# GpSimd's products of sample histories with taps, first five convolution blocks, set behind the issues of the adding transfers of low parts

## The chip, the core and the metric

The kernel runs on one core of one Trainium2 chip. The core has five engines that run beside each other and wait for one another through semaphores: TensorE (PE in the profile; its weight loads are a row of their own, PEld), VectorE (DVE), ScalarE (ACT), GpSimd (POOL) and SyncE (SP, which here only issues transfers). Sixteen DMA engines move the data. The metric is the time of one execution on the device in microseconds; the time of a kernel is the median of several runs.

## What is computed

One step of a decoder layer over 288 tokens: 256 of a prompt and 8 sequences of 4 new tokens, which carry a history. The part of the reference that the change touches is the depthwise convolution of width 31 over the gated projection; for the samples it runs over 30 tokens of history and the 4 new ones.

```python
h = rmsnorm(x, norm1_g)
proj = einsum("btd,de->bte", h, w_in) + b_in          # 2048 -> 3072
a, gate, z = proj[..., :1024], proj[..., 1024:2048], proj[..., 2048:]
u = a * sigmoid(gate)
u_ext = concatenate([hist_conv, u], axis=1)
c = silu(layernorm(depthwise_causal_conv(u_ext, conv_w, conv_b), ln_g, ln_b))
d = multiscale_pool(concatenate([hist_pool, z], axis=1), pos0)
p = einsum("btgc,gce->btge", d, pool_w) * pool_scale
x = x + einsum("btm,md->btd", concatenate([c, p]), w_out)
h2 = rmsnorm(x, norm2_g)
x = x + einsum("btf,fd->btd", square(relu(einsum("btd,df->btf", h2, w_ff1))), w_ff2)
y = rmsnorm(x, norm_f)
```

## The kernel before

**Products in three parts.** Channels lie on the 128 partitions, the 288 tokens along the free axis. A product in float32 is made from three products of halves: weight and activation are split into a high part (a cast to float32r) and a low part (value minus high part), and `gemm` (L296) adds high x high, low x high and high x low in a PSUM bank. A block of 256 weight columns over 2048 rows so takes 16 x 2 x 3 = 96 matmuls of 128x288. All of them are issued at L291, in the order of the program.

**Stages.** The projection goes by blocks in the order of `SEQUENCE` (L45): convolution blocks c0 to c7 (128 columns of a and 128 of the gate each), pool blocks p3 to p0, and small pool products P3 to P0 between them. c0 and c1 run together first, then c2, c3, c4, p3, c5 and so on. Then come the product with `w_out`, and four rounds of the feed-forward part.

**Weights.** `load` (L164) issues a transfer of 128x4x256 weights into a `wr` tile on SP's queue; six such tiles rotate. `split_part` (L254) makes the two parts: ScalarE casts the tile to `whi` (L260), and the low part `wlo` is made in one of three ways. V: VectorE subtracts (L265). G: GpSimd subtracts, in two halves (L268). D: ScalarE writes the negated high part into `wlo` (L262), and GpSimd issues a transfer that reads the weights again from device memory and adds them onto it (L263), the adding transfer of this text. `whi` and `wlo` have five buffers each. `WAYS` (L73) deals the ways out, four tiles to a block: c2 GVGV, c3 GDGG, c4 GDGD, p3 GDDG, c5 GDGD; the other blocks have no D. There are thus seven adding transfers; this text calls them D1 (c3, second tile), D2 and D3 (c4, second and fourth), D4 and D5 (p3, second and third), D6 and D7 (c5). Of a block's 96 matmuls the first 24 use the first tile, the next 24 the second, and so on; the first use of a tile's low part is the third of its 24.

**The convolution.** `conv_pair` (L427) scales the two banks of a block by the row of norms, makes u, and then, at a far lower priority (`later`, L111), the convolution: for the prompt one ScalarE instruction and 30 steps on VectorE (L445, L448); for the samples GpSimd multiplies all 8 x 4 windows with the 31 taps in one instruction (L451, 128x992, into a `prd` tile, two of which rotate), and VectorE sums them (L453). The results `c` are needed only by the layer norm, whose mean `ln_mean` (L549) enters the matmuls within the `w_out` stage.

**What sets the order.** Each engine runs its instructions in a fixed order, which a scheduler draws up from the dependencies and priorities. `tc.issue_after(x)` makes the scheduler set what is inside behind the instruction `x`. On GpSimd the subtractions, the issues of D1 to D7, the tap products and the pool sums stand in one such row, so a transfer is not issued before the instruction ahead of it has ended.

**Reordered heads.** At eight places (the first block, c2, c5, and later ones) `gemm` gets `classes=`, a string of zeros and ones (`TURN`, L70, 48 of them): it takes the next matmul of the head whose row parity is the digit, so the head's matmuls run in another order. Elsewhere the parity alternates.

Of the kernel before, what the change touches and what calls it, by code (L numbers as in the profile page):

```python
# [12 lines left out]
ALU = mybir.AluOpType  # L13
# [3 lines left out]
P = 128  # L17
D = 2048
SEQ = 256
NB, NS = 8, 4  # L20
# [4 lines left out]
CW = 31  # L25
# [61 lines left out]
def trunk_kernel(ctx: ExitStack, tc: tile.TileContext, io):  # L87
# [3 lines left out]
    nc = tc.nc  # L91
# [14 lines left out]
    def nm(s):  # L106
        seen[s] = seen.get(s, 0) + 1
        return f"{s}{seen[s]}"

    @contextmanager  # L110
    def later(by=LATER):  # L111

        tc.cur_priority += by
        yield
        tc.cur_priority -= by
# [18 lines left out]
    def f32(t):  # L134
        return t.bitcast(F32)
# [5 lines left out]
    def windows(ap, n):  # L141

        (step, parts), (far, groups), (near, size) = ap.ap
        return bass.AP(ap.tensor, ap.offset, [[step, parts], [far, groups], [near, size - n + 1], [near, n]])

    def samples(ap, n):
        return ap.rearrange("p (b t) -> p b t", t=n)
# [8 lines left out]
    def v(key, j):  # L156
        return vec[:, OFF[key] + j : OFF[key] + j + 1]
# [91 lines left out]
        last = mm(psum[:, 0, :T], minus, total, start=True, stop=True)  # L249
        return row_of(psum, psum[:, 0, :T], *args), last  # L250

    turns = {}

    def split_part(raw, src, hi, lo, way):  # L254

        nc.scalar.copy(hi, raw)  # L260
        if way == "D":
            nc.scalar.activation(lo, f32(hi), AF.Copy, scale=-1.0)  # L262
            nc.gpsimd.dma_start(lo, src, accum_op=ALU.add)  # L263
        elif way == "V":
            nc.vector.tensor_tensor(lo, raw, f32(hi), op=ALU.subtract)  # L265
        else:
            for j in range(0, raw.shape[1], 2):
                nc.gpsimd.tensor_tensor(lo[:, j : j + 2, :], raw[:, j : j + 2, :], f32(hi[:, j : j + 2, :]), op=ALU.subtract)  # L268
# [7 lines left out]
    def split(halves, stage="ff"):  # L276

        parts = []
        for raw, src in halves:
            turns[stage] = turns.get(stage, -1) + 1  # L280
            parts.append(spl())
            ways = WAYS.get(stage) or WAYS[stage[0]]
            split_part(raw, src, *parts[-1], ways[turns[stage] % len(ways)])
        return lambda k, m: columns(*parts[k // 4], k % 4, m)
# [88 lines left out]
    def pool_weights(g):  # L373
        raw, (hi, lo) = load_pool(g), spl()
        split_part(raw[:, 0:2, :], None, hi[:, 0:2, :], lo[:, 0:2, :], "V")
        return lambda k, m: columns(hi, lo, k, m)
# [35 lines left out]
    rb = row("rb")  # L412


    cs, pcs = [], []
    sum_c = tmpp.tile([P, 2, T], F32, name="sum_c", tag="ag2", bufs=2)

    def history(i):
# [8 lines left out]
    def conv_pair(i, banks):  # L427
        up = u_all[:, i, 0:UO]
        us = samples(u_all[:, i, UO:UL], US)
        ta, gate = [b[:, :T] for b in banks]  # L430
        for b in (gate, ta):
            nc.vector.tensor_tensor(b, b, rb, op=ALU.mult)
        tg = tmpp.tile([P, 2, T], F32, name=nm("tg"), tag="ag", bufs=2)[:, 0, :]
        nc.scalar.activation(tg, gate, AF.Sigmoid, bias=v("b_in", 8 + i))
        for out, a, b in ((up[:, CH:UO], ta[:, :SEQ], tg[:, :SEQ]), (us[:, :, CH:US], samples(ta[:, SEQ:T], NS), samples(tg[:, SEQ:T], NS))):
            nc.vector.scalar_tensor_tensor(out=out, in0=a, scalar=v("b_in", i), in1=b, op0=ALU.add, op1=ALU.mult)
        if i % 2 == 0:
            cs.append(actp.tile([P, 2, T], F32, name=nm("c"), tag="c", bufs=4))
        c = cs[i // 2][:, i % 2, :]
        with later():  # L440
            if i % 2 == 0:
                pcs.append(cvp.tile([P, 2, SEQ], F32, name=nm("pc"), tag="cv"))
            pc = pcs[i // 2][:, i % 2, :]
            cwv = vec[:, CWO + i * CW : CWO + (i + 1) * CW]
            nc.scalar.activation(pc, up[:, 0:SEQ], AF.Identity, bias=v("conv_b", i), scale=cwv[:, 0:1])  # L445
            for w in range(1, CW):
                dst = pc if w < CW - 1 else c[:, 0:SEQ]
                nc.vector.scalar_tensor_tensor(out=dst, in0=up[:, w : w + SEQ], scalar=cwv[:, w : w + 1], in1=pc, op0=ALU.mult, op1=ALU.add)  # L448
            prd = prdp.tile([P, NB, NS, CW + 1], F32, name=nm("prd"), tag="prd")
            nc.scalar.activation(prd[:, :, :, CW], ones[:, 0 : NB * NS].rearrange("p (b t) -> p b t", t=NS), AF.Identity, bias=v("conv_b", i), scale=0.0)  # L450
            nc.gpsimd.tensor_tensor(prd[:, :, :, 0:CW], windows(us, CW), cwv[:, None, None, :].to_broadcast([P, NB, NS, CW]), op=ALU.mult)  # L451
            cso = c[:, SEQ:T]
            nc.vector.tensor_reduce(samples(cso, NS), prd, axis=AX.X, op=ALU.add)  # L453
            if i % 2 and 1 < i < N8 - 1:
                for m in range(2):
                    nc.gpsimd.tensor_tensor(sum_c[:, m, :], (cs[0] if i == 3 else sum_c)[:, m, :], cs[i // 2][:, m, :], op=ALU.add)
            if i == N8 - 2:
                for part in (sum_c[:, 1, :], c):
                    nc.gpsimd.tensor_tensor(sum_c[:, 0, :], sum_c[:, 0, :], part, op=ALU.add)
# [54 lines left out]
    third = conv_products(2, classes=TURN)  # L514
    nc.gpsimd.memset(z_all[:, :, 0:PH], 0.0)
    conv_pair(0, pair0)
    conv_pair(1, pair1)
    conv_pair(2, third)
    def ahead(n):

# [61 lines left out]
    for j, c in enumerate(cs):  # L582
        n = tmpp.tile([P, 2, T], F32, name=nm("n"), tag="ag", bufs=2)
        nc.vector.tensor_tensor(n, c, norm["rows"][:, None, :].to_broadcast([P, 2, T]), op=ALU.mult)
        for m in range(2):
            i = 2 * j + m
# [195 lines left out]
```

## Time and profile before

| | |
|---|---|
| median of 3 runs | 1081.95 us (1081.67 to 1083.03) |
| profiled execution | 1082.43 us, of which its span 1080.6 us |
| granted TensorE clock | 0.998 |
| instructions in the span | 19528 |
| adding transfers | 7, of 512 KB each |
| tap products on GpSimd | 8, of 128x992 |

The span is the time from the first to the last instruction; the 1.83 us between it and the execution's time lie around it. Rows of the trace give a start in microseconds from the span's beginning, a duration, the engine, the line, the operation with its tiles, and a count; in square brackets stands how long the engine idled just before, and what ended that.

### The profile page before, as it was taken

How to read it: one execution, taken by the hardware profiler on the slowest of the kernel's cores; microseconds unless marked ns; L12 is line 12 of the kernel's file. 1: busy time of each engine (PE TensorE's matmuls, PEld its weight loads, DVE VectorE, ACT ScalarE, POOL GpSimd, SP SyncE). 2: the span in 40 equal slices, each digit the busy share in tenths (PEclk: the TensorE clock that was granted, in tenths of full speed). 3: DMA queues.
4: the chain of work that ended last, by engine and by line, in shares of the span. 5: the costliest groups of instructions: out<-in, count | busy, mean ns of one | idle time of the engine just before them, and what ended most of it. 6: DMA issues, size and time to landing. Idle time of an engine off the chain costs nothing.

```text
span 1080.6 us, 19528 instructions
## 1 busy us (share of the span) xinstructions
PE 1069.2 (99%) x8176; PEld 1067.9 (99%) x8176; DVE 633.7 (59%) x810; ACT 479.0 (44%) x588; POOL 175.9 (16%) x182
## 2 busy tenths in 40 slices
PE   9999999999999999999999999999999999999996
PEld 8999999999999999999999999999999999999996
DVE  7899999788654544444554444555544445554553
ACT  8654445665544433334443333444433334444441
POOL 0878979512000000000000000000000000000001
PEclk9999999999999999999999999999999999999999
DMA  9896478555555555555555555555555555555522
GB/s 326 288 263 182 145 187 247 177 171 173 162 173 166 169 175 163 170 173 165 170 174 164 170 170 167 171 173 162 173 168 167 173 171 164 173 166 170 172 79 88
DMA packets 58296, 190.71 MB, mean 176 GB/s; under 512 B 6240, under 2 KB 11232, under 8 KB 58208
## 3 DMA queue, kind: packets, MB, share of 16 engines
q1 hardware_dynamic: 56336, 184.35, 54.3%
q0 software_dynamic: 1008, 3.67, 1.9%
q8 instruction: 64, 1.05, 0.4%
q10 hardware_dynamic: 864, 1.44, 0.4%
q14 instruction: 24, 0.20, 0.0%
HBM read 185.16 MB, written 4.28 MB: 175 GB/s over the span
## 4 chain that ended last, share of the span: by engine, by line
PE 75%; issue 21%; ACT 2%; POOL 1%; DMA 1%; SPq 0%; POOLq 0%; DVE 0%
PE ac L291 74%; POOL wlo L268 1%; DMA wr<-in_w 1%; ACT whi L349 1%; PE pp L291 1%; DMA wlo<-in_w 1%; ACT hx L354 0%; ACT z_all L405 0%; POOL prd L451 0%; POOL xT L718 0%; ACT whi L260 0%; SPq L191 0%; POOLq L768 0%; DVE xT L691 0%; ACT whi L356 0%
## 5 line engine op out<-in xcount | busy, mean ns | idle before, releaser
L260 ACT CAST whi<-wr 128x1024 fp32r<-128x1024 f32 (+1 forms) x332 | 346.5, 1044 | 551.3 <-PE ac L291 536.7
L265 DVE TENSOR_TENSOR wlo<-wr,whi 128x1024 fp32r<-128x1024 f32 x288 | 353.5, 1227 | 348.1 <-ACT whi L260 348.1
L291 PE MATMUL ac<-ax,whi 128*128 128x288 f32 x2048 | 351.0, 292 | 0.0
L291 PE MATMUL ac<-fx,whi 128*128 128x288 f32 x2048 | 350.2, 292 | 0.0
L291 PEld LDWEIGHTS ac<-ax,whi 128*128 128x128 f32 x2048 | 296.0, 187 | 0.0
L291 PEld LDWEIGHTS ac<-fx,whi 128*128 128x128 f32 x2048 | 295.6, 187 | 0.0
L291 PE MATMUL ac<-ax,wlo 128*128 128x288 f32 x1024 | 217.3, 292 | 0.0
L291 PE MATMUL ac<-fx,wlo 128*128 128x288 f32 x1024 | 216.4, 292 | 0.0
L291 PEld LDWEIGHTS ac<-ax,wlo 128*128 128x128 f32 x1024 | 162.5, 187 | 0.0
L291 PEld LDWEIGHTS ac<-fx,wlo 128*128 128x128 f32 x1024 | 162.2, 187 | 0.0
L291 PE MATMUL ac<-hx,whi 128*128 128x288 f32 x768 | 131.9, 296 | 1.4 <-DVE hx L352 1.4
L718 POOL TENSOR_TENSOR xT<-xT,rf 128x288 f32<-128x288 f32 x4 | 3.1, 795 | 799.9 <-ACT rf L722 799.9
L291 PEld LDWEIGHTS ac<-hx,whi 128*128 128x128 f32 x768 | 112.6, 190 | 1.8 <-ACT hx L354 1.7
L268 POOL TENSOR_TENSOR wlo<-wr,whi 128x512 fp32r<-128x512 f32 x74 | 102.4, 1433 | 17.1 <-ACT whi L260 16.0
L448 DVE SCALAR_TENSOR_TENSOR pc<-u_all,vec,pc 128x256 f32<-128x256 f32 x232 | 99.3, 479 | 1.9 <-ACT pc L445 0.7
L291 PE MATMUL ac<-hx,wlo 128*128 128x288 f32 x384 | 80.4, 295 | 0.2 <-DMA wlo<-in_w 0.2
L291 PEld LDWEIGHTS ac<-hx,wlo 128*128 128x128 f32 x384 | 61.1, 189 | 0.4 <-DMA wlo<-in_w 0.4
L291 PE MATMUL ac<-dx,whi 128*128 128x288 f32 x256 | 46.8, 295 | 0.0
L291 PE MATMUL ac<-mx,whi 128*128 128x288 f32 x256 | 44.9, 293 | 0.0
L660 DVE SCALAR_TENSOR_TENSOR t<-ac,r 128x576 f32<-128x576 f32 x32 | 24.2, 757 | 25.4 <-PE ac L291 25.3
L291 PEld LDWEIGHTS ac<-dx,whi 128*128 128x128 f32 x256 | 38.4, 188 | 0.2
L291 PEld LDWEIGHTS ac<-mx,whi 128*128 128x128 f32 x256 | 37.5, 188 | 0.2 <-DVE xT L579 0.2
(129 smaller groups left out, 529.6 us busy)
## 6 DMA issues: line engine op xcount, KB each, us to landing
wr<-in_w SPq DMA_DIRECT2D x335, 512.0 KB, 3.8
wlo<-in_w POOLq DMA_DIRECT2D x7, 512.0 KB, 7.8
xT<-in_xT SPq DMA_DIRECT2D x8, 288.0 KB, 7.7
wr<-in_w SPq DMA_DIRECT2D x5, 256.0 KB, 3.9
out_u_out<-u_all SPq DMA_DIRECT2D x1, 1208.0 KB, 9.6
u_all<-in_hist_c SPq DMA_DIRECT2D x8, 136.0 KB, 5.3
out_z_out<-z_all SPq DMA_DIRECT2D x1, 668.0 KB, 9.2
z_all<-in_hist_p SPq DMA_DIRECT2D x4, 152.0 KB, 6.6
```

Source lines behind the costliest of these rows:

```text
L260: nc.scalar.copy(hi, raw)
L265: nc.vector.tensor_tensor(lo, raw, f32(hi), op=ALU.subtract)
L268: nc.gpsimd.tensor_tensor(lo[:, j : j + 2, :], raw[:, j : j + 2, :], f32(hi[:, j : j + 2, :]), op=ALU.subtract)
L291: last = nc.tensor.matmul(*args, **kw)
L349: nc.scalar.copy(hi[:, blocks[0]], raw[:, blocks[0]])
L448: nc.vector.scalar_tensor_tensor(out=dst, in0=up[:, w : w + SEQ], scalar=cwv[:, w : w + 1], in1=pc, op0=ALU.mult, op1=ALU.add)
L660: nc.vector.scalar_tensor_tensor(out=t, in0=bk[:, :, :T], scalar=0.0, in1=both(rows2[0]), op0=ALU.max, op1=ALU.mult)
L718: eng.tensor_tensor(xk, xk, r[:, None, :].to_broadcast([P, n, T]), op=ALU.mult)
```

## The change

The list `added` collects the issues of the adding transfers. The tap products of block i are set behind one of them by `issue_after`: those of c0 and c1 behind D1, that of c2 behind D2, those of c3 and c4 behind D4. Since D2 and D4 have to exist by then, the emission of the convolution of c2 and c3 is put off by one block (`waiting`); the body of `conv_pair` from L439 on becomes the function `taps`. Nothing is computed otherwise than before.

```diff
-    turns = {}
+    turns, added = {}, []
...
-            nc.gpsimd.dma_start(lo, src, accum_op=ALU.add)
+            added.append(nc.gpsimd.dma_start(lo, src, accum_op=ALU.add))
...
-    cs, pcs = [], []
+    cs, pcs, waiting = [], [], []
...
+        while waiting:
+            taps(*waiting.pop())
+        if i in (2, 3):
+            waiting.append((i, up, us))
+        else:
+            taps(i, up, us)
+
+    def taps(i, up, us):
+
         c = cs[i // 2][:, i % 2, :]
         with later():
...
-            nc.gpsimd.tensor_tensor(prd[:, :, :, 0:CW], windows(us, CW), cwv[:, None, None, :].to_broadcast([P, NB, NS, CW]), op=ALU.mult)
+            with tc.issue_after(added[max(0, min(3, 2 * i - 3))].ins):
+                nc.gpsimd.tensor_tensor(prd[:, :, :, 0:CW], windows(us, CW), cwv[:, None, None, :].to_broadcast([P, NB, NS, CW]), op=ALU.mult)
```

Lines behind L439 move down by up to ten (L268 and L263 keep their numbers, L451 becomes L461), and the numbers of the tiles of c4 and later blocks change with the order of emission. The first place is GpSimd's row around the first adding transfer. Before, with `wlo_604` and `wlo_609` the low parts of c3's first two tiles, `wlo_618` and `wlo_623` those of the other two, and `prd_667` and `prd_708` the products of c0 and c1:

```order
L268 TENSOR_TENSOR wlo_604<-wr_599,whi_603 128x512 x2
L451 TENSOR_TENSOR prd_667<-u_all,vec 128x32x31
L451 TENSOR_TENSOR prd_708<-u_all,vec 128x32x31
L263 DMA wlo_609<-in_w 128x1024
L268 TENSOR_TENSOR wlo_618<-wr_613,whi_617 128x512 x2
L268 TENSOR_TENSOR wlo_623<-wr_615,whi_622 128x512 x2
```

In the changed kernel the same stretch of GpSimd reads:

```order
L268 TENSOR_TENSOR wlo_604<-wr_599,whi_603 128x512 x2
L263 DMA wlo_609<-in_w 128x1024
L461 TENSOR_TENSOR prd_667<-u_all,vec 128x32x31
L461 TENSOR_TENSOR prd_708<-u_all,vec 128x32x31
L268 TENSOR_TENSOR wlo_618<-wr_613,whi_617 128x512 x2
L268 TENSOR_TENSOR wlo_623<-wr_615,whi_622 128x512 x2
```

D1 has moved ahead of two tap products. The second place follows directly on GpSimd: before, the four tiles of c4 (`wlo_858` to `wlo_877`, D2 and D3 among them), the first three of p3 (`wlo_1027`, then D4 and D5) and the products of c2 and c3 (`prd_751`, `prd_918`):

```order
L268 TENSOR_TENSOR wlo_858<-wr_853,whi_857 128x512 x2
L451 TENSOR_TENSOR prd_751<-u_all,vec 128x32x31
L263 DMA wlo_863<-in_w 128x1024
L268 TENSOR_TENSOR wlo_872<-wr_867,whi_871 128x512 x2
L263 DMA wlo_877<-in_w 128x1024
L268 TENSOR_TENSOR wlo_1027<-wr_1022,whi_1026 128x512 x2
L451 TENSOR_TENSOR prd_918<-u_all,vec 128x32x31
L263 DMA wlo_1032<-in_w 128x1024
L263 DMA wlo_1041<-in_w 128x1024
```

The same rows of the changed kernel, where the tiles have the numbers 822 to 841 for c4, 990 to 1004 for p3, and 883 and 1051 for the products of c2 and c3:

```order
L268 TENSOR_TENSOR wlo_822<-wr_817,whi_821 128x512 x2
L263 DMA wlo_827<-in_w 128x1024
L461 TENSOR_TENSOR prd_883<-u_all,vec 128x32x31
L268 TENSOR_TENSOR wlo_836<-wr_831,whi_835 128x512 x2
L263 DMA wlo_841<-in_w 128x1024
L268 TENSOR_TENSOR wlo_990<-wr_985,whi_989 128x512 x2
L263 DMA wlo_995<-in_w 128x1024
L461 TENSOR_TENSOR prd_1051<-u_all,vec 128x32x31
L263 DMA wlo_1004<-in_w 128x1024
```

D2 and D4 have each moved ahead of one tap product; D3 and D5 stand where they stood, and so do the products of c4 and later blocks. TensorE's order is the same in both kernels, and SP's too but for one output transfer that moves by one place. ScalarE and VectorE run the same instructions with a few swaps of neighbours and another interleaving of the convolution's steps: VectorE runs six steps instead of three before the first sum over a `prd` tile.

## The prediction

> **What bounds the kernel now.** I began with the page's busy times and the list of TensorE's waits.
>
> ```profile
> PE 1069.2 (99%) x8176; PEld 1067.9 (99%) x8176; DVE 633.7 (59%) x810; ACT 479.0 (44%) x588; POOL 175.9 (16%) x182
> PE ac L291 <- DVE hx L352: 1.4, 1, 1.4
> PE warm L214 <- DVE cst L231: 1.0, 1, 1.0
> PE ac L291 <- DMA wlo<-in_w: 0.2, 1, 0.2
> ```
>
> TensorE is busy 99% of the span and waits three times in all. Two of the waits are at the start; the third is for an adding transfer. GpSimd, whose row the change edits, is busy 16%, so its own time is worth nothing; only what it issues can matter. The chain of work that ended last says where:
>
> ```profile
> 44.41 5.97 DMA wlo<-in_w
> 50.38 0.04 issue
> 50.42 60.24 PE ac L291 x454
> ...
> 171.50 26.61 PE ac L291 x204
> ...
> 282.86 572.63 PE ac L291 x4404
> ```
>
> From 50.42 us on the chain is TensorE alone, and just ahead of it stands D1, issued at 44.41 and landed at 50.38. Whatever brings that matmul forward brings the end forward, as long as nothing else becomes late. TensorE's rows around the wait:
>
> ```profile
> 48.77 0.68 PE L291 MATMUL ac<-hx,whi 128*128 128x288 f32 x4
> ...
> 49.55 0.68 PE L291 MATMUL ac<-hx,whi 128*128 128x288 f32 x4
> 50.42 0.54 PE L291 MATMUL ac<-hx,wlo 128*128 128x288 f32 x2 [0.20 <-DMA wlo<-in_w]
> 50.80 0.69 PE L291 MATMUL ac<-hx,whi 128*128 128x288 f32 x4
> 51.59 0.70 PE L291 MATMUL ac<-hx,whi 128*128 128x288 f32 x4
> 52.39 0.70 PE L291 MATMUL ac<-hx,whi 128*128 128x288 f32 x4
> ```
>
> Two things are to be seen. Rows overlap, since matmuls are pipelined, so I read starts and not durations. Ahead of the wait, four high and two low matmuls pass between 48.77 and 49.55: 0.78/6 = 130 ns each. The next one was due at 49.55 + 4 x 0.13 = 50.07 and came at 50.42; it and its neighbour then took 0.38 instead of 0.26. The wait so costs 0.35 + 0.12 = **0.47 us**, more than the 0.20 that the idle time shows. And behind it the step is 0.80 (51.59 to 52.39): 133.3 ns per matmul. The wait has put TensorE into another rhythm. How long this lasts, the view by stages tells (busy time, count, granted clock, share of the DMA engines, GB/s):
>
> ```profile
> 42.00:49.80 7.80, 7.80 (x62) 1.00 0.62 155
> 52.00:84.00 32.00, 32.00 (x243) 1.00 0.97 261
> 95.00:127.00 32.00, 32.00 (x248) 1.00 0.50 156
> 127.00:159.00 32.00, 32.00 (x249) 1.00 0.57 167
> 175.00:191.00 16.00, 16.00 (x125) 1.00 0.84 225
> ```
>
> A window also counts two or three matmuls that stick out at its edges: 32/0.1333 = 240 (243 counted), 32/0.130 = 246 (248). All stages read 100% busy at a granted clock of 1.00, and yet the one behind the wait does fewer matmuls. The slow rhythm ends at c5, whose head is reordered.
>
> **The change, part by part.** GpSimd's row, the waits in brackets, and the two ScalarE rows that write what D1 and D2 add onto:
>
> ```profile
> 37.65 2.55 POOL L268 TENSOR_TENSOR wlo<-wr,whi 128x512 fp32r<-128x512 f32 x2 [2.21 <-ACT whi L260]
> 40.16 4.33 POOL L451 TENSOR_TENSOR prd<-u_all,vec 128x992 f32<-128x992 f32 x2
> 44.41 1.01 POOL L263 DMA_DIRECT2D wlo<-in_w  x1
> 45.21 7.75 POOL L268 TENSOR_TENSOR wlo<-wr,whi 128x512 fp32r<-128x512 f32 x6
> 52.71 2.42 POOL L451 TENSOR_TENSOR prd<-u_all,vec 128x992 f32<-128x992 f32 x1
> 54.86 1.11 POOL L263 DMA_DIRECT2D wlo<-in_w  x1
> ...
> 63.76 2.16 POOL L451 TENSOR_TENSOR prd<-u_all,vec 128x992 f32<-128x992 f32 x1
> 65.99 0.88 POOL L263 DMA_DIRECT2D wlo<-in_w  x1
> 68.90 0.87 POOL L263 DMA_DIRECT2D wlo<-in_w  x1 [2.04 <-ACT wlo L262]
> 39.26 1.06 ACT L262 ACTIVATE wlo<-whi 128x1024 fp32r<-128x1024 f32 x1
> 51.09 1.06 ACT L262 ACTIVATE wlo<-whi 128x1024 fp32r<-128x1024 f32 x1
> 64.38 1.06 ACT L262 ACTIVATE wlo<-whi 128x1024 fp32r<-128x1024 f32 x1
> 67.54 1.06 ACT L262 ACTIVATE wlo<-whi 128x1024 fp32r<-128x1024 f32 x1
> ```
>
> *D1.* ScalarE has its part ready at 39.26 + 1.06 = 40.32, GpSimd is free at 40.20. In the new order the issue goes out at about 40.4, 4.0 us sooner. How long the seven adding transfers take to land:
>
> ```profile
> DMA to landing us min/median/max: 6.0/7.8/10.2
> ```
>
> D1's own 5.97 gives a landing at 46.4, the longest 50.6; the need is at 50.07. The shortest is D1's, at a DMA share of 0.62 (row 42.00:49.80), and its new place lies mostly in the same stretch, so I take 46.4: 3.7 us of slack, and the wait goes. That removes 0.47 us.
>
> *The rhythm.* The matmul at 50.42 is the 27th of c3's 96 (the first low one of its second tile), the one at 50.80 the 29th. From there 68 are left of c3, and 96 each of c4 and p3: 260 matmuls run at 133.3 ns before c5's reordered head, which so begins at 50.80 + 34.66 = 85.46; at 130 ns they save 260 x 3.33 ns = **0.87 us**. Bounds for this term: 0, if the slow rhythm came from something else, and 0.87. The row 42.00:49.80 (62 matmuls, 7.8/0.13 = 60 and two at the edges) shows c2 and the head of c3 running at 130 until the wait and only until it, so I take 0.87.
>
> *Tap products of c0 and c1* start at about 41.4 instead of 40.16 and end near 45.7. Behind them stand the low parts of c3's third tile, done 0.4 us later than before, about 48.2; their first use by TensorE is its third tile's third matmul, 50.07 + 24 x 0.13 = 53.19. Those 5 us hide the delay. VectorE's sums over the products come later too, but with more steps of the convolution ahead of them, and only the layer norm's mean needs them. Both cost nothing.
>
> *D2 and D4* go out one product earlier: D2 when GpSimd has done c4's first tile, at about 53.3 (52.71, and the half microsecond by which the six subtractions now end later) instead of 54.86, D4 at about 65.4 instead of 65.99, since ScalarE's part is ready only at 65.44. *D3 and D5* go out as before, D5 behind ScalarE's 67.54 + 1.06. None of the four is waited for now, so no time is removed. But TensorE now comes sooner and could meet them; that is the first rival.
>
> *VectorE* is the next engine that could be late, as it carries the convolution up to the layer norm's mean.
>
> ```profile
> 85.66 0.76 DVE L470 TENSOR_TENSOR tz<-ac,rb 128x576 f32<-128x576 f32 x1 [0.90 <-PE ac L291]
> ...
> 195.26 0.46 DVE L553 TENSOR_TENSOR sum_c<-pmean,c 128x288 f32<-128x288 f32 x1
> ...
> 197.96 0.65 PE L291 MATMUL pmean<-sum_c,ones 128*128 128x288 f32 x2
> ```
>
> It ends the sum at 195.72, 2.2 us before TensorE takes it up, more than the whole gain; and at 85.66 it idles 0.90 for TensorE, so it will follow when TensorE comes sooner. The cover holds.
>
> **Sum:** 0.47 + 0.87 = 1.34 us. Against the profiled execution's own 1082.43 (span 1080.6 and 1.83 around it) that is 1081.1. That execution is 0.48 above the median of the runs, 1081.95; the same gain taken from the median gives **1080.6 us**.
>
> **A rule against the second term.** In the rows above TensorE makes 130 and 133.3 ns per matmul at one granted clock of 1.00. The Trainium skill, "TensorE: Matmul & The Clock Gate", section "Back-to-back issue gap", gives one isolated gap for a warm clock, columns/2.4 + 2.5 ns, for 288 columns 122.5 (an estimate from that page), with no second rhythm. By that rule a wait costs its gap and no more, and the sum would be 0.47 us. The trace disagrees with it as far as the two rates go. What remains of the rule is that the slow rhythm might follow from something other than the wait; that is a rival below.
>
> **The rivals.**
>
> *The gain is given back at p3.* The rows of D4 and D5 alone:
>
> ```profile
> DMA to landing us min/median/max: 9.8/9.8/9.8
> DMA to landing us min/median/max: 10.2/10.2/10.2
> ```
>
> D5 lands at 68.90 + 10.2 = 79.1. p3 starts at 50.80 + (68 + 96) x 0.1333 = 72.7, and needs D5 with its 51st matmul, at 72.7 + 50 x 0.1333 = 79.3: 0.2 us of slack now. In the new order the need is at 50.07 + (70 + 96 + 50) x 0.13 = 78.15. ScalarE works at TensorE's pace here, which at 67.5 is ahead by 0.47 and (67.5 - 50.8)/0.1333 x 3.33 ns = 0.42, so D5's issue moves by about 0.9 to 68.0, and D5 would land at 78.2 if it took 10.2 again. For a shorter time speaks that D1 and D2 have left the crowded stretch (0.97 of the DMA engines between 52 and 84) by 4.0 and 1.6 us. Against it, that the stretch stays nearly full and TensorE draws on it 2.5% faster. If D5 were 0.6 late, the wait and 46 matmuls of slow rhythm (0.15) would come back: 1081.4.
>
> *One rhythm.* Only the gap goes: 1081.95 - 0.47 = 1081.5.
>
> *The change doesn't do what it says.* D1 takes 10.2 at its new place, lands at 50.6, and the wait stays: 1082.0.
>
> *Slower: the reordered head of c5.* It now finds TensorE in the slow rhythm and leaves it in the fast one. In the changed kernel it would find the fast rhythm. If it turned that into the slow one, the rest up to the next reordered head, in the `w_out` stage near 171.5, would run at 133.3: from 84.1 to 171 are some 660 matmuls; the 610 behind the 48 of the head x 3.33 ns are 2.03 us lost, less 1.34 gained, **1082.6**. It decides at c5's head and nowhere else. Against it: the head near 171.5 is itself entered in the fast rhythm (row 127.00:159.00) and left in it (row 175.00:191.00, 16/0.13 = 123 and two at the edges). The same mishap at the last reordered head, near 283, would cost at least the 4404 matmuls of the chain's row x 3.33 ns = 14.7 us, about 1095, but nothing of the change reaches that place except a start 1.3 us sooner.
>
> **How the numbers follow.** Forecast 0.60; given back at p3 0.19; one rhythm 0.07; D1 late all the same 0.04; c5's head turns the rhythm 0.06; a later head turns it 0.03; something more gained, such as a later short wait of TensorE, 0.01. The predicted time is the forecast's, 1080.6. The three runs lie from 0.28 below to 1.08 above their median; with as much below the forecast, and up to the case of c5's head with the runs' spread, the range is 1079.5 to 1082.9. A measurement of this kernel can tell about 0.2%, 2.2 us, from no change: below 1079.8 or above 1084.1. Nearly all the cases lie between. Faster by that much 0.06 (the forecast with a favourable spread), within it 0.89, slower 0.05 (the late head, and a little of c5's).
>
> **What would show it.** In the changed kernel's profile, TensorE's list of waits should have no adding transfer; D1's issue should stand near 40.4 and its landing near 46.4, with the tap products behind it. The window 52 to 84 should count 248 matmuls, not 243, and c5 should begin near 84.1 instead of 85.5. The mean's matmul should come 1.3 us before 197.96. A wait near 75 or 78 for `wlo` would show the first rival; a count of 243 in the windows from 95 to 159 the last. Wrong altogether I would be if a wait stood between 84 and 171 where there is none now, or if the stage behind 283 ran at another rate.

## The result

| | before | changed |
|---|---|---|
| median | 1082.37 us (8 runs, 1081.67 to 1083.5) | 1085.99 us (8 runs, 1084.63 to 1086.24) |
| ratio | | 1.003, 95% interval 1.002 to 1.004 |
| profiled execution's span | 1080.6 us | 1084.2 us |

The changed kernel is slower by 3.6 us, where 1.3 us of gain were forecast. TensorE's list of waits in the changed kernel (microseconds in total, times, longest) names the places:

```profile
PE ac L291 <- DVE hx L352: 1.5, 1, 1.5
PE ac L291 <- DMA wlo<-in_w: 1.4, 1, 1.4
PE warm L214 <- DVE cst L231: 1.0, 1, 1.0
PE ac L291 <- DVE dx L512: 0.9, 1, 0.9
PE pp L291 <- DVE dx L500: 0.5, 1, 0.5
PE pp L291 <- ACT dx L499: 0.3, 1, 0.3
PE ac L291 <- DVE wlo L358: 0.2, 1, 0.2
```

Two of them stood there before, at the start, and the last, of 0.2, lies there too. A wait for an adding transfer is still there, but longer, and three waits are new: for `dx`, the split input of the small pool products and, behind them, of the pools' part of the `w_out` product, which VectorE and ScalarE make. GpSimd's row shows that D1 did what it was to do:

```profile
40.76 1.05 POOL L263 DMA_DIRECT2D wlo<-in_w  x1 [1.48 <-issue]
41.56 4.62 POOL L461 TENSOR_TENSOR prd<-u_all,vec 128x992 f32<-128x992 f32 x2
45.84 7.81 POOL L268 TENSOR_TENSOR wlo<-wr,whi 128x512 fp32r<-128x512 f32 x6
53.34 1.15 POOL L263 DMA_DIRECT2D wlo<-in_w  x1
```

D1 goes out at 40.76 and the wait for it is gone. The wait in the list is for D2, as TensorE's rows around it show:

```profile
60.35 0.68 PE L291 MATMUL ac<-hx,whi 128*128 128x288 f32 x4
60.87 0.42 PE L291 MATMUL ac<-hx,wlo 128*128 128x288 f32 x2
61.13 0.68 PE L291 MATMUL ac<-hx,whi 128*128 128x288 f32 x4
63.19 0.54 PE L291 MATMUL ac<-hx,wlo 128*128 128x288 f32 x2 [1.38 <-DMA wlo<-in_w]
63.56 0.69 PE L291 MATMUL ac<-hx,whi 128*128 128x288 f32 x4
```

Ahead of it six matmuls take 0.78 (60.35 to 61.13), 130 ns each; the next was due at 61.65 and came at 63.19. The view by stages (length, busy time with the count of matmuls, granted clock, DMA share, GB/s) in the changed kernel:

```profile
42.00:49.80 7.80, 7.80 (x62) 1.00 0.59 152
52.00:84.00 32.00, 30.62 (x232) 1.00 0.97 259
95.00:127.00 32.00, 32.00 (x249) 1.00 0.52 157
127.00:159.00 32.00, 32.00 (x249) 1.00 0.45 142
175.00:191.00 16.00, 16.00 (x123) 1.00 0.90 244
```

The stretch from 52 to 84 counts 232 matmuls, where 248 were forecast and 243 stood before. To set kernels beside each other I take TensorE's starts of two matmuls: those of c2's and c5's first matmul (384 matmuls apart, 49.9 us at 130 ns), and from c5's first to the 8000th matmul. The time up to c2 is left out, as it differs from profile to profile (c2 began between 32.68 and 34.44 in the fifteen of them, at 34.11 before and 33.21 in the changed kernel), although the engines run the same order up to there. By these two numbers the changed kernel's profile loses 0.87 us early (52.22 instead of 51.35) and 3.59 late (967.66 instead of 964.07). All kernels of this study, in us; each ratio is against runs of the kernel before made together with it (medians 1081.65 to 1082.37), and the last two columns are from one profile each:

| kernel | median | ratio to before, 95% interval | c2 to c5 | c5 to 8000th |
|---|---|---|---|---|
| before | | | 51.35 | 964.07 |
| changed | 1085.99 | 1.003 [1.002, 1.004] | 52.22 | 967.66 |
| d1_alone | 1086.13 | 1.0044 [1.0032, 1.0056] | 53.00 | 967.66 |
| d2_alone | 1082.10 | 1.0005 [0.9996, 1.0013] | 51.30 | 964.07 |
| early_new_late_old | 1083.80 | 1.0019 [1.0009, 1.0028] | 51.74 | 964.05 |
| early_old_late_new | 1085.22 | 1.0034 [1.0021, 1.0047] | 51.12 | 967.62 |
| all_gates_late_old | 1081.33 | 0.9993 [0.9985, 1.0002] | 50.92 | 964.07 |
| two_moved | 1084.68 | 1.0026 [1.0016, 1.0036] | 50.63 | 967.15 |
| pool_first | 1087.48 | 1.0053 [1.0040, 1.0065] | 50.94 | 969.33 |
| meet_less | 1083.82 | 1.0016 [1.0007, 1.0025] | 51.59 | 965.39 |
| meet_fewer | 1082.84 | 1.0013 [1.0005, 1.0022] | 51.28 | 965.51 |
| hole_filled | 1082.12 | 1.0006 [0.9993, 1.0019] | 51.67 | 964.72 |
| hole_half | 1081.50 | 0.9997 [0.9988, 1.0006] | 50.37 | 964.75 |
| half_and_gates | 1082.62 | 1.0007 [0.9998, 1.0016] | 51.32 | 965.88 |
| half_less | 1081.77 | 1.0004 [0.9994, 1.0014] | 50.02 | 965.36 |

The two columns are not equally firm. The changed kernel, all_gates_late_old, two_moved, pool_first, meet_less and meet_fewer run the same order up to c5, but for one swap of neighbours on VectorE near 66, and yet their profiles take 50.63 to 52.22 from c2 to c5, 51.26 on average. Against the 51.35 of before that is no loss, but nothing of the 1.34 us forecast either. The late column repeats to a few hundredths where the order is the same, and its 3.59 is the size of the medians' 3.6.

The late loss sits at P1, the small pool product at 160, and at the first head of `w_out`:

```profile
160.13 0.42 PE L291 MATMUL ac<-hx,whi 128*128 128x288 f32 x2
160.85 0.53 PE L291 MATMUL pp<-dx,whi 128*128 128x288 f32 x2 [0.30 <-ACT dx L499]
161.22 0.43 PE L291 MATMUL pp<-dx,wlo 128*128 128x288 f32 x2
162.19 0.79 PE L291 MATMUL pp<-dx,whi 128*128 128x288 f32 x4 [0.54 <-DVE dx L500]
...
170.00 0.43 PE L291 MATMUL ac<-dx,wlo 128*128 128x288 f32 x2
171.30 0.79 PE L291 MATMUL ac<-dx,whi 128*128 128x288 f32 x4 [0.88 <-DVE dx L512]
```

The three waits show 1.72 us; each costs, as D1's did, some 0.27 more than it shows; and from the first of them to the mean's matmul, some 290 matmuls on, TensorE is in the slow rhythm, 290 x 3.33 ns = 0.97. That is 3.5 of the 3.59. VectorE has become late: it scales p1's bank at 141.44 instead of 138.15, with the p2 bank scaled at 111.65 in both. Why, the two kernels' rows of VectorE and GpSimd in between show. In the changed kernel:

```profile
117.05 3.52 POOL L268 TENSOR_TENSOR wlo<-wr,whi 128x512 fp32r<-128x512 f32 x2
117.34 2.07 DVE L265 TENSOR_TENSOR wlo<-wr,whi 128x1024 fp32r<-128x1024 f32 x1
125.03 3.00 POOL L268 TENSOR_TENSOR wlo<-wr,whi 128x512 fp32r<-128x512 f32 x2
125.09 1.78 DVE L494 SCALAR_TENSOR_TENSOR d<-s,z_all 128x512 f32<-128x512 f32 x1 [0.32 <-POOL s L493]
130.54 2.20 POOL L461 TENSOR_TENSOR prd<-u_all,vec 128x992 f32<-128x992 f32 x1 [1.24 <-DVE u_all L436]
130.76 2.59 DVE L500 TENSOR_TENSOR dx<-d,dx 128x576 fp32r<-128x576 f32 x1
141.44 0.74 DVE L480 TENSOR_TENSOR tz<-ac,rb 128x576 f32<-128x576 f32 x1
```

And before (L484 and L490 are the changed kernel's L494 and L500):

```profile
117.02 3.53 POOL L268 TENSOR_TENSOR wlo<-wr,whi 128x512 fp32r<-128x512 f32 x2
118.13 1.26 DVE L265 TENSOR_TENSOR wlo<-wr,whi 128x1024 fp32r<-128x1024 f32 x1
128.05 0.69 DVE L484 SCALAR_TENSOR_TENSOR d<-s,z_all 128x512 f32<-128x512 f32 x1 [0.96 <-POOL s L483]
129.60 2.21 POOL L451 TENSOR_TENSOR prd<-u_all,vec 128x992 f32<-128x992 f32 x1
131.44 0.99 DVE L490 TENSOR_TENSOR dx<-d,dx 128x576 fp32r<-128x576 f32 x1
138.15 0.74 DVE L470 TENSOR_TENSOR tz<-ac,rb 128x576 f32<-128x576 f32 x1
```

The same three instructions of VectorE take 2.07, 1.78 and 2.59 instead of 1.26, 0.69 and 0.99, together 3.5 us more. VectorE runs them in another order among the steps of the convolution, and each now comes up soon after GpSimd has begun an instruction. Look at the ends: GpSimd's product ends at 130.54 + 2.20 = 132.74, and `dx` at 133.35, 0.61 later; before, the product ended at 131.81 and `dx` at 132.43, 0.62 later. VectorE's instruction so ends a fixed time after GpSimd's, as if it had started only when that was through. I call this a meeting. The meetings aren't all: between the scalings of the two banks VectorE also runs 35 steps of the convolution instead of 33, which at 0.39 us a step is another 0.8, while it idles 0.43 instead of 1.22. TensorE's order is the same in both kernels, and GpSimd does the same work: what has moved VectorE is the scheduler, which drew up another order for it from block p3 on, presumably since the changed row of GpSimd altered what was ready when.

### The profile page after: what moved, and what is told of

Its sections match the earlier page's. It is cut to its first block, busy times and chain, and to the rows that moved or that the text cites. A ratio compares the mean times of both kernels' runs of the same rounds, so it can differ in the third digit from the quotient of the medians.

```text
span 1084.2 us, 19528 instructions
## 1 busy us (share of the span) xinstructions
PE 1069.5 (99%) x8176; PEld 1067.1 (98%) x8176; DVE 637.4 (59%) x810; ACT 478.5 (44%) x588; POOL 176.2 (16%) x182
## 4 chain that ended last, share of the span: by engine, by line
PE 65%; issue 21%; DVE 5%; POOL 4%; DMA 2%; ACT 1%; SPq 0%; POOLq 0%; ACTq 0%; DVEq 0%
PE ac L291 65%; DVE pc L457 3%; POOL wlo L268 2%; DMA wr<-in_w 1%; POOL s L489 1%; DMA wlo<-in_w 1%; DVE wlo L265 1%; ACT hx L354 0%; ACT z_all L405 0%; DVE dx L500 0%; ACT whi L349 0%; DVE c L463 0%; DVE d L494 0%; POOL prd L461 0%; POOL xT L728 0%
## 5 line engine op out<-in xcount | busy, mean ns | idle before, releaser
L265 DVE TENSOR_TENSOR wlo<-wr,whi 128x1024 fp32r<-128x1024 f32 x288 | 354.5, 1231 | 348.4 <-ACT whi L260 348.4
L268 POOL TENSOR_TENSOR wlo<-wr,whi 128x512 fp32r<-128x512 f32 x74 | 102.6, 1441 | 16.3 <-ACT whi L260 15.5
```

## The experiments

Theory A is the account above. Its parts to be tested: that the order from p3 on makes the late loss, that D1's gain is lost at D2, and that meetings make VectorE late.

**d1_alone and d2_alone** take the change apart. Against the changed kernel:

```diff
-        if i in (2, 3):
+        if False:
...
-            with tc.issue_after(added[max(0, min(3, 2 * i - 3))].ins):
+            with tc.issue_after(added[0].ins) if i < 2 else nullcontext():
```

> Only the products of c0 and c1 are set behind D1; D2 and D4 stay behind the products as before, and nothing is put off. Theory A (VectorE's order from p3 on is another one, it meets GpSimd more often, and TensorE waits for it at P1; what D1 gains early is lost again at D2): 1086, ratio 1.002 to 1.004, VectorE's scaling of p2 starts near 141.4 and TensorE waits for dx at 160 to 161. Rival B (the earlier issues of D2 and D4 in the crowded stretch cost the time): 1082.4 or less. Rival C (D1 ahead of the products costs the time by itself, early): 1086 with c5 starting later than 85.5.

For d2_alone the condition is `added[1].ins` with `i == 2`, and the emission is put off for block 2 alone.

> Only the product of c2 is set behind D2, the order of the other engines is that of before. Theory A: 1082.4 (ratio 0.999 to 1.001); D2 is issued near 53.3 instead of 54.9, and lands near 62.7 all the same, since the weight loads ahead of it have to be through first. Rival B: 1084 or more. If D2 followed its issue, it would land near 61.2.

(The bank scaled at 141.4, in this and in a later expectation, is p1's.) D1 alone makes the whole loss, with the same three waits for `dx` and 967.66 from c5 on; D2 alone changes nothing. Rival B falls. Rival C's sign, c5 later than 85.5, is there as well (86.17, behind a wait of 2.2 for D2), so this pair doesn't decide between A and C. How late D2 lands is told by its own row, from issue to landing, in the changed kernel and in d2_alone:

```profile
DMA to landing us min/median/max: 9.8/9.8/9.8
```

```profile
DMA to landing us min/median/max: 8.8/8.8/8.8
```

Before it was:

```profile
DMA to landing us min/median/max: 7.8/7.8/7.8
```

Before, D2 was issued at 54.86 and landed at 62.7; in d2_alone it was 53.37 and 62.1, in the changed kernel 53.34 and 63.1. As c2 began at 34.11, 34.44 and 33.21, I count from there: issued at 20.8, 18.9 and 20.1, landed at 28.6, 27.7 and 29.9. An issue 1.8 sooner bought 0.9 in d2_alone, and one 0.6 sooner landed 1.4 later in the changed kernel.

**early_new_late_old and early_old_late_new** write the orders of VectorE, GpSimd and ScalarE out by hand, as lists of instruction names, each instruction set behind the one before it on its engine. The computation and TensorE's order are untouched:

```diff
+    placed = {i.name: i for i in tc.nc.cur_bb.bb.instructions}
+    for order in ORDERS:
+        for a, b in zip(order, order[1:]):
+            tc.add_manual_dep(placed[f"I-{b}"], f"I-{a}", mybir.DependencyInfo(mybir.DependencyClass.NoSync, mybir.DependencyReason.DATA), reason="issue_after")
```

Each list is that of d1_alone up to the scaling of p3's bank and that of before from there on, or the other way round.

> D1 ahead of the products of c0 and c1, with the orders of VectorE, GpSimd and ScalarE up to p3's scaling as they come with it; from there on all three have the order of before. Theory A: 1082.0 to 1082.6 (what D1 gains is lost at D2, nothing is lost later), no wait for dx near 160, ratio 0.998 to 1.001. Rival C: 1086.

> The other way round: up to p3's scaling the orders of before, with D1 behind the products; from there on the orders of the changed kernel. Theory A: 1086, ratio 1.002 to 1.004, VectorE's scaling of p2 near 141.4, waits for dx at 160 to 161. Rival C: 1082.4.

This settles the late loss: with the new order from p3 on it is 967.62 to 967.66 whatever came first (changed, d1_alone, early_old_late_new), with the old one 964.05 to 964.07 (before, d2_alone, early_new_late_old). Rival C falls as far as the late part goes. The median of early_new_late_old missed its expectation: its twelve runs lie between 1081.01 and 1085.9, seven above 1083.5, and the profiled one at 1081.95. What made those seven longer isn't known; none of them was profiled. Its early order, D1 ahead of the products and D2 behind its own, is that of d1_alone, whose profile lost 1.65 up to c5 at D2, so D2's landing is a suspect.

**all_gates_late_old** is the same with D2 and D4 ahead of the products as well, so the changed kernel's whole early order:

```diff
 L268 TENSOR_TENSOR wlo_858<-wr_853,whi_857 128x512 x2
+L263 DMA wlo_863<-in_w 128x1024
 L461 TENSOR_TENSOR prd_751<-u_all,vec 128x32x31
-L263 DMA wlo_863<-in_w 128x1024
...
 L268 TENSOR_TENSOR wlo_1027<-wr_1022,whi_1026 128x512 x2
+L263 DMA wlo_1032<-in_w 128x1024
 L461 TENSOR_TENSOR prd_918<-u_all,vec 128x32x31
-L263 DMA wlo_1032<-in_w 128x1024
```

> As early_new_late_old, but with D2 and D4 ahead of the products too, so the whole early order of the changed kernel, and the later order of before. Theory A: from the start of c5 on 964.1 as before; from c2 to c5 51.3 to 53, according to how late D2 lands: 1081.5 to 1084. If a further cause works behind c5: more than 964.5 there.

No further cause works behind c5. So the change as it was meant comes to 0.9993 of before, with an interval that includes 1; the later order that came with it turns this into 1.003.

**two_moved** was the first test of the meetings: the changed kernel's orders with two of the three long VectorE instructions a little later.

```diff
+L512 SCALAR_TENSOR_TENSOR dx_1242<-pp_1539,vec,dx_1242 128x288
+L457 SCALAR_TENSOR_TENSOR pc_719<-u_all,vec,pc_719 128x256
 L265 TENSOR_TENSOR wlo_1691<-wr_1683,whi_1690 128x1024
-L512 SCALAR_TENSOR_TENSOR dx_1242<-pp_1539,vec,dx_1242 128x288
-L457 SCALAR_TENSOR_TENSOR pc_719<-u_all,vec,pc_719 128x256
...
-L500 TENSOR_TENSOR dx_1536<-d_1531,dx_1536 128x2x288
 L457 SCALAR_TENSOR_TENSOR pc_1057<-u_all,vec,pc_1057 128x256
 L457 SCALAR_TENSOR_TENSOR pc_1714<-u_all,vec,pc_1714 128x256
 L457 SCALAR_TENSOR_TENSOR pc_1057<-u_all,vec,pc_1057 128x256
 L457 SCALAR_TENSOR_TENSOR pc_1714<-u_all,vec,pc_1714 128x256
+L500 TENSOR_TENSOR dx_1536<-d_1531,dx_1536 128x2x288
```

> The orders of the changed kernel, but for two instructions of VectorE: p2's dx (2.59 us beside GpSimd's product) four convolution steps later, and one low part (2.07 us beside GpSimd's subtraction) two steps and one dx later. Theory A (these meetings with GpSimd make VectorE late at P1): each takes about 1 us, VectorE's scaling of p1's bank starts 2.0 to 2.5 us sooner than 141.4, the waits for dx at P1 go, and from the start of c5 to matmul 8000 it is 964.1 to 964.7 instead of 967.6: 1082.5 to 1083.5. If the place of these two doesn't matter: 967.6, and 1086.

A miss: from p2's scaling to p1's it is 29.83 instead of 29.79, and all waits stay. The rows of VectorE and GpSimd in two_moved say why:

```profile
129.57 2.20 POOL L461 TENSOR_TENSOR prd<-u_all,vec 128x992 f32<-128x992 f32 x1 [1.23 <-DVE u_all L436]
131.72 3.06 POOL L268 TENSOR_TENSOR wlo<-wr,whi 128x512 fp32r<-128x512 f32 x2
131.76 1.87 DVE L500 TENSOR_TENSOR dx<-d,dx 128x576 fp32r<-128x576 f32 x1
```

`dx` now comes up just as the product ends, and loses to the subtraction behind it; the low part fell beside GpSimd's next sum and took 2.12. A meeting that is moved is not removed. (The 0.51 us that two_moved gains behind c5 come from the rhythm: from 181 on TensorE is back at 130 ns, where the changed kernel stays at 133.3 up to the mean.)

**pool_first** asked whether it is enough to let VectorE do the pool path ahead of convolution steps:

```diff
+L480 TENSOR_TENSOR tz_1856<-ac_1753,rb_250 128x576
 L457 SCALAR_TENSOR_TENSOR pc_1714<-u_all,vec,pc_1714 128x256
 L457 SCALAR_TENSOR_TENSOR pc_1057<-u_all,vec,pc_1057 128x256
...
-L480 TENSOR_TENSOR tz_1856<-ac_1753,rb_250 128x576
```

and the same for p0's bank, `d`, `dx` and what follows up to c7's u.

> The orders of the changed kernel, but on VectorE the pool path comes ahead of convolution steps: the scaling of p1's bank 5 steps and a low part sooner, that of p0's bank and d 7 steps, p1's dx 4 steps, and what follows up to c7's u 6 steps. No work is taken away. Theory A (VectorE is late for TensorE at P1, P0 and the first head of w_out): these waits go. As VectorE still has 3.3 us more behind it, the mean's sum comes at 199.1 in the time of the changed kernel, and TensorE, which would take it up at 197.9, waits there for 1 to 1.5 us: from the start of c5 to matmul 8000 965.0 to 965.8 instead of 967.6; 1083.5 to 1084.5. If something other than VectorE's lateness costs the time: 967.6.

A miss again, and the slowest kernel of all: a low part that started at 139.44 beside GpSimd took 2.24, another at 146.30 took 1.66, and TensorE waits for `dx` four times. Putting the pool path ahead of the steps is not enough as long as its neighbours meet GpSimd.

**meet_less** therefore puts VectorE's instructions where GpSimd is idle or the steps can fill the time:

```diff
+L500 TENSOR_TENSOR dx_1536<-d_1531,dx_1536 128x2x288
 L436 SCALAR_TENSOR_TENSOR u_all<-ac_1584,vec,tg_1709 128x256
 L436 SCALAR_TENSOR_TENSOR u_all<-ac_1584,vec,tg_1709 128x8x4
 L457 SCALAR_TENSOR_TENSOR pc_1057<-u_all,vec,pc_1057 128x256
-L500 TENSOR_TENSOR dx_1536<-d_1531,dx_1536 128x2x288
...
-L265 TENSOR_TENSOR wlo_1899<-wr_1891,whi_1898 128x1024
 L457 SCALAR_TENSOR_TENSOR pc_1714<-u_all,vec,pc_1714 128x256
...
+L265 TENSOR_TENSOR wlo_1899<-wr_1891,whi_1898 128x1024
 L265 TENSOR_TENSOR wlo_1907<-wr_1902,whi_1906 128x1024
```

> The orders of the changed kernel, but VectorE's p2 dx comes just ahead of c6's u (so ahead of GpSimd's product), and two low parts come 5 and 0 steps later, between GpSimd's subtractions. Theory A with meetings as the cause of VectorE's lateness: dx takes 0.7 to 1.0 instead of 2.59, the second low part 1.2 instead of 1.63, VectorE's scaling of p1's bank starts 1.8 to 2.2 us sooner than 141.4 (against the start of c5: 54.0 instead of 56.0), the waits at P1 go for the most part: 965.0 to 966.4 from c5 to matmul 8000. If meetings only move (as in two_moved): 967 or more.

All of it came as expected by meetings. VectorE's rows in meet_less:

```profile
130.57 0.76 DVE L500 TENSOR_TENSOR dx<-d,dx 128x576 fp32r<-128x576 f32 x1 [0.22 <-ACT dx L499]
131.25 0.64 DVE L436 SCALAR_TENSOR_TENSOR u_all<-ac,vec,tg 128x256 f32<-128x256 f32 x2
131.80 5.31 DVE L457 SCALAR_TENSOR_TENSOR pc<-u_all,vec,pc 128x256 f32<-128x256 f32 x13
137.02 2.35 DVE L265 TENSOR_TENSOR wlo<-wr,whi 128x1024 fp32r<-128x1024 f32 x2
139.29 0.88 DVE L457 SCALAR_TENSOR_TENSOR pc<-u_all,vec,pc 128x256 f32<-128x256 f32 x2
140.08 0.75 DVE L480 TENSOR_TENSOR tz<-ac,rb 128x576 f32<-128x576 f32 x1
```

`dx` takes 0.76, each of the two low parts 1.2, and the thirteen steps 0.4 each though GpSimd runs its product beside them. With p2's bank scaled at 112.11 it is 27.97 to p1's, 1.82 less than in the changed kernel; the waits at P1 are gone, and 2.27 of the 3.59 us come back. Some 0.5 of the 2.27 is the rhythm, which came back in two_moved too, with all waits in place.

**meet_fewer** goes on with the other two long instructions (the low part two steps later, p2's `d` two steps later).

```diff
+L457 SCALAR_TENSOR_TENSOR pc_1057<-u_all,vec,pc_1057 128x256
+L457 SCALAR_TENSOR_TENSOR pc_719<-u_all,vec,pc_719 128x256
 L265 TENSOR_TENSOR wlo_1691<-wr_1683,whi_1690 128x1024
-L457 SCALAR_TENSOR_TENSOR pc_1057<-u_all,vec,pc_1057 128x256
...
+L432 TENSOR_TENSOR ac_1584<-ac_1584,rb_250 128x288
+L457 SCALAR_TENSOR_TENSOR pc_1057<-u_all,vec,pc_1057 128x256
 L494 SCALAR_TENSOR_TENSOR d_1531<-s_1528,z_all 128x2x256
-L457 SCALAR_TENSOR_TENSOR pc_1057<-u_all,vec,pc_1057 128x256
-L432 TENSOR_TENSOR ac_1584<-ac_1584,rb_250 128x288
```

> As meet_less, with the two other long meetings shortened: the low part that started 0.3 us behind a subtraction of GpSimd starts two steps later, and so does p2's d. Theory A in its sharper form (a VectorE instruction with two SBUF inputs ends 1.08, 0.55 or 0.62 us, by its size, after the instruction of GpSimd that runs when it comes up; its price is what is left of that): low part 1.26 instead of 2.08, d 1.0 instead of 1.76, together 1.5 to 1.6 saved; from the scaling of p2's bank to that of p1's 26.4 instead of 27.97; the wait for dx at the head of w_out goes: 964.1 to 964.5 from c5 to matmul 8000; 1081.6 to 1082.6. If the rest of the loss has another cause: 965.2 or more.

Half a miss. The low part took 1.29 as expected, but `d` still took 1.55, and the low part right behind it fell into GpSimd's next subtraction and took 1.78 instead of 0.68. From p2's scaling to p1's it is 28.09, and behind c5 965.51. The remaining 1.4 us are thus not shown to be meetings; the two convolution steps more ahead of p1's scaling (0.8 us of VectorE) are still there, and no run takes them out. What remains of TensorE's waits is one of 0.8 for a `dx` at the head of `w_out`.

**hole_filled and hole_half** were about D2. After D1 the DMA engines of the changed kernel are nearly idle from 46 to 50 (a share of 0.15), and I supposed that the weight loads ahead of D2 start late since GpSimd subtracts later. In hole_half:

```diff
 L263 DMA wlo_609<-in_w 128x1024
+L268 TENSOR_TENSOR wlo_618<-wr_613,whi_617 128x512 x2
 L461 TENSOR_TENSOR prd_667<-u_all,vec 128x32x31
 L461 TENSOR_TENSOR prd_708<-u_all,vec 128x32x31
-L268 TENSOR_TENSOR wlo_618<-wr_613,whi_617 128x512 x2
 L268 TENSOR_TENSOR wlo_623<-wr_615,whi_622 128x512 x2
```

In hole_filled both rows of subtractions stand ahead of the products; the later order is that of before.

> D1 first, then the four subtractions of c3's last two tiles, and only then the products of c0 and c1; from p3's scaling on the order of before. Theory A (D2 is late because the weight loads ahead of it are, and these wait for tiles that the subtractions free): the loads start 2 to 4 us sooner than in the changed kernel, D2 lands near 61, TensorE does not wait for it, and c2 to c5 takes 50.0 (384 x 0.13): 1080.5 to 1081.3. If D2's landing hangs on something else, it stays near 63 and c2 to c5 takes 51.3 or more: 1082 or more.

> As hole_filled, but with only the two subtractions of c3's third tile ahead of the products. Theory A: between the two: D2 lands near 62, c2 to c5 takes 50 to 51.5, 1080.8 to 1082.3.

hole_filled fails: D2 landed near 62 and TensorE waited 0.8 for it. In hole_half TensorE did not wait for it, and c2 to c5 took 50.37; but now 0.68 are lost behind c5, where TensorE waits for c7's u. So what makes D2 late is not settled. It is not the engines' order alone: d1_alone and early_new_late_old run the same one up to c5 and issued D2 21.6 behind c2's start, and it landed 30.7 and 28.4 behind it.

**half_and_gates and half_less** are tries at a kernel faster than both. Against hole_half, half_and_gates has D2 and D4 ahead of the products and four steps put behind c7's u; half_less has two instructions moved out of GpSimd's way:

```diff
-L494 SCALAR_TENSOR_TENSOR d_1531<-s_1528,z_all 128x2x256
 L436 SCALAR_TENSOR_TENSOR u_all<-ac_1584,vec,tg_1709 128x256
 L436 SCALAR_TENSOR_TENSOR u_all<-ac_1584,vec,tg_1709 128x8x4
 L457 SCALAR_TENSOR_TENSOR pc_1057<-u_all,vec,pc_1057 128x256
+L494 SCALAR_TENSOR_TENSOR d_1531<-s_1528,z_all 128x2x256
...
+L457 SCALAR_TENSOR_TENSOR pc_1057<-u_all,vec,pc_1057 128x256
+L457 SCALAR_TENSOR_TENSOR pc_1714<-u_all,vec,pc_1714 128x256
 L494 SCALAR_TENSOR_TENSOR d_1868<-s_1865,z_all 128x2x256
-L457 SCALAR_TENSOR_TENSOR pc_1057<-u_all,vec,pc_1057 128x256
-L457 SCALAR_TENSOR_TENSOR pc_1714<-u_all,vec,pc_1714 128x256
```

> A try at a kernel faster than both: hole_half with D2 and D4 ahead of the products of c2 and c3, the later order of before, and four convolution steps put behind c7's u, for which hole_half waited. Theory A: c2 to c5 50.0 to 50.6, from c5 on 964.1: 1080.0 to 1081.0. If VectorE is late elsewhere instead: 964.6 or more, 1081.5.

> hole_half with two meetings less behind c5: p2's d comes behind c6's u and one step (it had VectorE wait 0.96 for GpSimd), p1's d two steps later. Theory A: VectorE gains 0.5 to 1.5 us, the wait of 0.4 for c7's u goes, and what hole_half has gained early stays: 964.1 from c5 on instead of 964.75; 1080.6 to 1081.3. If VectorE is not what hole_half waited for: 964.7.

Neither is faster than before. half_and_gates waits 1.0 for a `dx` in the `w_out` stage. half_less is instructive: early its profile gains all there is to gain, 51.35 - 50.02 = 1.33, and it loses 1.29 behind c5. TensorE's only wait there in its rows:

```profile
169.78 0.37 PE L291 MATMUL ac<-dx,whi 128*128 128x288 f32 x1 [0.43 <-DVE u_all L436]
```

The wait is the same in hole_half, and in hole_filled, which gained nothing early:

```profile
170.49 0.37 PE L291 MATMUL ac<-dx,whi 128*128 128x288 f32 x1 [0.42 <-DVE u_all L436]
```

```profile
170.93 0.37 PE L291 MATMUL ac<-dx,whi 128*128 128x288 f32 x1 [0.39 <-DVE u_all L436]
```

All three stand at the same matmul, 86.4 to 86.6 us behind c5's start, whether the kernel lost 0.32 early (hole_filled) or gained 0.98 (hole_half) or 1.33 (half_less). So the wait does not come from TensorE's being sooner. VectorE is late by these kernels' own early order: it scales p3's bank 1.1 to 1.2 us behind c5's start, where before and all_gates_late_old have 0.2, and has c7's u ready 86.3 to 86.4 behind it instead of 85.54. That half_less loses 0.61 more than hole_half is the rhythm: behind the same wait it counts 122 matmuls from 179 to 195, hole_half 125. In all_gates_late_old, 0.43 us sooner than before, c7's u is ready 85.54 behind c5's start as before: there VectorE follows TensorE in full. Whether a gain of 1.33 can be had without this early order, and kept, stays open.

## Why the prediction was wrong

- *D1* came nearly as forecast: issued at 40.76 (40.4), its wait gone, c3 in 12.48 us (45.79 to 58.27), 96 x 0.13. But it took 7.3 to land instead of the 5.97 assumed, at 48.1 and not 46.4, with the need at 45.79 + 26 x 0.13 = 49.17: 1.1 us of slack, not 3.7.
- *The sum* of 0.47 and 0.87 was of the right size for what nothing disturbs: half_less has its 1.33 from c2 to c5. In the changed kernel the fast rhythm lasted until 61.65 and came back only at c5, whose head turned it as before (249 matmuls in the windows from 95 and from 127). Over the six profiles with its early order the gain up to c5 averages 0.1, not 1.34.
- *D2 and D4*: "None of the four is waited for now, so no time is removed" was right of before, and the first rival said that TensorE could meet them, but it was worked out for D5 alone. It came at D2. D2's row was there to be used: it landed at 62.70, while the 27th matmul of c4 was due at 59.86 + 26 x 0.1333 = 63.3, and in the new order at 50.07 + 96 x 0.13 = 62.55. Only the earlier issue kept it clear, 53.3 + 7.8 = 61.1. The term that was mis-sized is D2's landing: 9.8 us behind its issue, and 9.0 to 9.9 in the six profiles. In the changed kernel's it cost 1.54 us at 63.19 and the rhythm behind it.
- *Tap products*, "Both cost nothing", and *VectorE*, "The cover holds": this is the step that failed, and by itself turns the sign. The cover was read from the times of before as if VectorE's order stayed. The order of the changed kernel was there to be read, and only its early part was: VectorE's sequence differs from p3's scaling on. It is worth 3.6 us by the six profiles of the first experiments, 1.8 to 2.27 of them through meetings with GpSimd (meet_less, without and with the rhythm); two more convolution steps ahead of p1's scaling are the likely part of the rest, not shown by a run. That VectorE "will follow when TensorE comes sooner" held, as all_gates_late_old shows. But the cover was taken at the mean alone, 2.2 us, while VectorE is needed sooner at p1's `dx` and at c7's u, which before was ready at 171.00 for a matmul at 171.34.
- *The rivals*: c5's head did not turn slow, and the late head near 283 didn't either. None of them had VectorE late. The prediction's own sign of being wrong altogether, a wait between 84 and 171 where there was none, is what stands there at 160.85 and 162.19.
- *The rule against the second term*, one gap and no second rhythm, does not hold here: behind D2's wait, too, TensorE makes fewer matmuls at a granted clock of 1.00 (232 in 52 to 84, where the wait of 1.4 would account for 11 less than 248).

## What to carry to other kernels

When an edit goes through a scheduler, compare the whole order of every engine up to the point where the stages no longer differ, not only the place of the edit: here one transfer moved ahead on GpSimd changed how VectorE's work fell beside GpSimd's 70 us later, and that was the result. Take no gain of a microsecond from one profile: with one and the same early order it was 50.63 to 52.22 us from c2 to c5. When TensorE is brought forward, list everything it takes up in the next 100 us with the slack of each, and expect the smallest to bind. And for each VectorE instruction with both inputs in SBUF (where the tiles lie, other than the PSUM banks of the matmuls), look at what GpSimd runs when it comes up, and put steps that read PSUM there instead.

## What the runs showed of the hardware

VectorE and GpSimd shut each other out, and the price can be read from two rows. GpSimd pays too: the two subtractions at 117.05 took 3.52 us around VectorE's low part, where two took 2.54 at 133.47 in meet_fewer with only convolution steps beside them. In the fifteen profiles, between 84 and 172 us, 229 VectorE instructions with two SBUF inputs (low parts at L265, `d`, `dx`) came up while an instruction of GpSimd was running. All but one ended a nearly fixed time after that instruction's end, wherever they had come up in it: low parts of 1024 columns 1.08 to 1.19 us, of 512 columns 0.54 to 0.64, `d` 0.55, `dx` 0.61 to 0.73. Alone they took 1.21, 0.68, 0.68 and 0.75. So the price of a meeting is what is left of GpSimd's instruction: up to 1.3 us of a subtraction, up to 2.2 of a product. The one exception, 1.86, is two_moved's `dx`, which came up 0.01 before the product's end and had the next subtraction served first. Convolution steps, which read one input from PSUM, ran at 0.4 beside the product (meet_less). The Trainium skill, "SBUF — State Buffer", section "Who interferes with whom", says this: a VectorE instruction with two SBUF inputs contends with a GpSimd instruction that reads SBUF, and whichever issues first has the shared pair of ports for the whole instruction. The traces agree, with the numbers above.

The other surprise is how little an adding transfer's issue says of its landing. In the fifteen profiles D2 took 5.9 to 9.9 us from the one to the other: the earliest issue, 52.5 (all_gates_late_old), landed at 61.7, the latest, 55.3 (hole_half), at 61.2. D1 likewise: counted from c2's start it was issued at 10.3 in the three kernels that keep it behind the products and landed at 16.0 to 16.3; in the twelve others it was issued at 6.8 to 7.6 and landed at 14.8 to 15.2. Why is open.
